# The second score product of the 64-feature heads on all 128 rows of the systolic array

## The chip, the cores and the metric

The kernel runs on one core of a Trainium2 chip. The metric is the device time of one execution in microseconds. The kernel before took 1842.69 us, the median of three runs (1839.75 to 1848.87).

## The reference

Two transformer blocks on 512 tokens of 1024 features, in 32-bit floating point. The first has four attention layers, the second a layer of four mixers, a gated feed-forward part and a last gated projection. What matters here are the scores of heads with 64 features: the sliding-window layer (16 heads), the forgetting layer (16 heads), the two attention mixers of the second block (4 heads each), and the index of the sparse attention (8 heads of 64 features that share one key).

```python
def _swa_branch(x, w_in, sinks, w_out):                    # SWA_HEAD_DIM = 64
    ...
    s = jnp.einsum('bqnkgd,bnskd->bnkgqs', q, kb, preferred_element_type=jnp.float32) * scale
    ...
def _dense_causal(q, k, v, scale, cum=None):               # forgetting layer: FOX_HEAD_DIM = 64
    ...
        s = jnp.einsum('bqhd,bkhd->bhqk', q_blk, k, preferred_element_type=jnp.float32) * scale
    ...
def dsa_mixer(q, k, v, iq, ik, iw, bias_tab):              # index: IDX_HEADS = 8, IDX_DIM = 64
    ...
        sc = jax.nn.relu(jnp.einsum("bqhd,bsd->bqhs", iqc, ik32))
        score = jnp.einsum("bqh,bqhs->bqs", iwc, sc) * idx_scale
    ...
        _, sel = lax.top_k(score, topk)                    # 128 keys of each query
```

## The kernel before, in words

Every number is split into a high part in the rounded 32-bit format that TensorE takes, and a low part, the remainder. A product of two split operands is three matmuls: high by high, high by low, low by high (`mm3`, lines 156 to 158). Activations stand feature by row: 128 features on the 128 rows, 512 tokens as columns.

A head of 64 features fills half the rows, so two of the three products share one matmul. `split_q` stacks the query of a head as high part and low part, on 64 rows each. `split_k` stacks the high part of the key twice. The first matmul of `qk_mm` (line 231) works on all 128 rows and gives high by high plus low by high. The second (line 232) gives high query by low key, and reads only the 64 rows of the high query (`r`) and of the low key. The index does the same by itself in lines 885 and 886. One score tile has 128 queries and 128 to 512 keys, so each tile takes two matmuls, and both load the same query columns as stationary operand.

The low keys lie in different places: in the sliding-window layer twice in a tile of the ring `qk` (`both=True`); in the forgetting layer once, two heads stacked, in one half of the tile `kl2` of the tag `kr`, the halves taking turns by pair of heads; in the mixers in a ring `kl` of two tiles; for the index in two tiles of `ik`. The ring `qk` has 7 tiles in the first block and also holds query and key tiles, biases (`b`) and the second half of the output weights at a layer's end.

`attend` runs one head: the score tiles go to PSUM (ring `s`, two banks), VectorE adds the bias and takes the row maxima (L396), ScalarE takes the exponential (L412), VectorE normalises (L420), TensorE transposes (L436), the result is split (L183, L184) and multiplied by the values (L445). `pairs` issues the projections of the next pair of heads ahead of the two heads at hand, so TensorE has projections (L156 to L158 into `ps_acc`) to put between the steps of the heads. In the mixers, `tick` puts 48 steps of the top-128 selection (L911, L912) into VectorE's program.

Each engine executes its list in order. The lists are written by a scheduler at build time that replays its own estimate of times, so a change of a size or of a buffer moves rows of all lists. GpSimd (POOL) takes the low parts of the weights (L138) and small steps of the norms (L318).

Of the kernel before, what the change touches and what calls it, by code (L numbers as in the profile page):

```python
# [9 lines left out]
F32 = mybir.dt.float32  # L10
R = mybir.dt.float32r
# [47 lines left out]
# output projections of the four layers and of the mixers (and of the end): PSUM banks by halves of the columns and  # L59
# token tiles, and the order of the blocks, 4 * half + tile  # L60
# [15 lines left out]
class Act:  # L76
    """Feature-major activation split exactly in two float32r parts, units of 4 blocks of 128 features."""
# [11 lines left out]
class Kern:  # L89
# [27 lines left out]
    def phase(s, ctx, tags):  # L117
        """a pool that lives as long as ctx, with its tags."""
        s.phase_pool = ctx.enter_context(s.tc.tile_pool(name="ph", bufs=1, reuse_waits="tile"))
        s.phase_tags = tags  # L120
# [9 lines left out]
    def w(s, W, k0, kn, c0, cn, th="wh", tl="wl", dve=False):  # L130
        """weights split in two parts."""
# [9 lines left out]
    def w_heads(s, W, k, c0, a, b):  # L141
        """weights of 4 heads with a + b columns each, one k tile: columns ordered [4 x a | 4 x b]."""
# [17 lines left out]
    def proj(s, W, c0, m, a, tag="acc"):  # L160
        """out^T block: (W[:, c0:c0+m])^T a."""
        out = s.p(tag)
        for u in range(0, a.n, 4):
            kn = min(4, a.n - u)
            h, l = s.w(W, u, kn, c0, m)
            for k in range(kn):
                s.mm3(out[:m], h[:, k], l[:, k], a.h(u + k), a.l(u + k), u + k == 0, u + k == a.n - 1)
        return out

    def proj_multi(s, blocks, a):  # L170
        """as proj for several (W, c0, m, tag), by halves of the tokens, so that the first halves can start before the
        second half of a is there."""
# [13 lines left out]
    def split_heads(s, ps, extra):  # L186
        """two heads of 64 rows each: a tile [high and low part] per head with the head in rows 0..63; extra(e) -> rows
        that follow, of both parts or of the high one."""
# [8 lines left out]
    def split_q(s, ps):  # L197
        """two heads of 64 rows each, stacked: [high of 0; low of 0] and [low of 1; high of 1]."""
# [10 lines left out]
    def split_k(s, ps, both=False, kl=None):  # L209
        """two heads of 64 rows each: the high part of each twice, [0; 0] and [1; 1], and the low parts [0; 1], or  # L210
        twice each like the high parts."""
        nc = s.nc
        k = s.t("qk", [P, 2, S], R)
        if both:
            kl = s.t("qk", [P, 2, S], R)
        elif kl is None:
            kl = s.t("kl", [P, S], R)
        for e, (h, l) in enumerate(HALF):
            nc.scalar.copy(k[h, e], ps[h])
            nc.scalar.copy(k[l, e], ps[h])  # L220
            low = kl[h, e] if both else kl[h]
            nc.vector.tensor_sub(low, ps[h], k[h, e].bitcast(F32))  # L222
# [4 lines left out]
    def qk_mm(s, out, i, k0, q, e, kd, kl):  # L227
        """scores of 64-row heads: (high + low of q) . high of k, and high of q . low of k."""
        mm = s.nc.tensor.matmul
        c, kk, r = slice(i * P, (i + 1) * P), slice(k0 * P, (i + 1) * P), HALF[e][0]  # L230
        mm(out, q[:, e, c], kd[:, kk], start=True, stop=False)  # L231
        return mm(out, q[r, e, c], kl[r, kk], start=False, stop=True)  # L232

# [1 line left out]
    def to_T(s, x, t, a, grp=(0, 1)):  # L235
        """token tile t of x (token-major) into a (feature-major, split)."""
# [8 lines left out]
    def bcast_row(s, row, tag):  # L245
        """a row of DRAM on every partition."""
# [5 lines left out]
    def out_units(s, W, n, half):  # L252
        """split weights of half the columns, one k tile each, in whatever is free at the end of a layer."""
# [5 lines left out]
    def pair_units(s, W, n, c0, cn, dve=False):  # L259
        """split weights of cn columns, one k tile each, both parts in a tile of the attention."""  # L260
# [15 lines left out]
    def out_proj(s, W, o, evac, banks=None, oi=5, split_last=False):  # L276
        """token-major o @ W by halves of the columns; evac(t, half, psum)."""
# [61 lines left out]
    def rms_T(s, x, t, g, a):  # L339
        """rmsnorm(x) * g of token tile t into a."""  # L340
# [9 lines left out]
    def stage_end(s, W, o, g_post, g_next, out_proj=None):  # L350
        """x += rmsnorm(o @ W) * g_post; returns rmsnorm(x) * g_next."""
# [31 lines left out]
    def attend(s, s_mm, k0s, bias, scale, v, sink=None, shift=None):  # L383
        """s_mm(out, i, k0): scores of query tile i against keys from tile k0; v(j) -> stationary [P, 128] of key
        tile j; returns the PSUM tile with the two halves of the output."""
# [65 lines left out]
    def join(s, og, e, o):  # L451
        """two halves of a head's output summed into rows 64e.. of og."""
# [97 lines left out]
    def latent(s, W, c0, n, m, g_row, xT, tag, rest=None):  # L550
        """rmsnorm of m columns of x @ W from c0 (feature-major, split); the columns up to n, transposed, into rest."""
# [27 lines left out]
    def pairs(s, order, prep, head, Wg, g0, xT, oT):  # L579
        """the pairs of heads in turn; the projections of the next pair come ahead of the two heads of one."""  # L580
# [26 lines left out]
    def v_split(s, ps, vts, f=0.5):  # L607
        """f times the token-major values of pairs of heads into [hi lo] per head; vts: [P, 2, 2, 64] per pair."""
# [10 lines left out]
    def v_proj(s, W, c0, n, a, evac, more="p", first=False):  # L619
        """token-major a @ W[:, c0:c0+n]; evac(t, psum); more: where weights wider than 256 columns go too."""  # L620
# [18 lines left out]
    def swa(s, j, li, xT, g_next):  # L639
# [8 lines left out]
        def prep(p):  # L648
# [6 lines left out]
            if pr == 0:  # L655
                K[kp] = s.split_k(kps, True)
# [16 lines left out]
    def fox(s, j, li, xT, g_next):  # L673
# [4 lines left out]
        kl2 = s.t("kr", [P, 2, S], R, name="kl2")  # L678
# [12 lines left out]
        # log sigmoid(z) = min(z, 0) - ln(1 + exp(-|z|))  # L691
# [22 lines left out]
        def prep(p):  # L714
# [17 lines left out]
            kt = s.split_k(kps or s.proj(Win, 1024 + p * P, P, xT), kl=kl2[:, p % 2])  # L732
            return qt, kt, V[g][pr], bs

        def head(d, p, e):
            q, (k, kl), v, bs = d
            return s.attend(lambda out, i, k0: s.qk_mm(out, i, k0, q, e, k[:, e], kl), [0] * T,
# [26 lines left out]
    def spill_x(s):  # L764
        """x to DRAM, for the layers whose attention needs its place."""
# [7 lines left out]
    def rel_rows(s):  # L773
        """per head 128 times the row w[511 - d] = 8 bias(d), -1e30 for the distances d < 0, in DRAM."""
# [13 lines left out]
    def rel_bias(s, h):  # L788
        """bias of head h (times 8) with the causal mask: [P, 512], key tiles i-3..i of query tile i; a row further
        down starts one element earlier."""  # L790
# [23 lines left out]
    def pool(s, W, hT, mix, b, before=None):  # L814
        """windows of one half of the channels; returns what completes it, to be called later."""
# [16 lines left out]
        # the first group of channels takes its window one doubling before the second  # L832
# [22 lines left out]
    def index_keys(s, W, hT):  # L855
        """keys and weights of the index of the sparse attention."""
        nc = s.nc
        ps, *s.iq = s.proj_multi([(W, 2304, 72, "acc"), (W, 1792, P, "acc"), (W, 1920, P, "acc")], hT)
        kh, kl = s.t("ik", [P, S], R), s.t("ik", [P, S], R)
# [13 lines left out]
    def index(s, W, hT, b):  # L873
        """what heads 2b and 2b + 1 of the index add to the scores."""
# [5 lines left out]
        for e in range(2):  # L880
            h = 2 * b + e
            for i in (1, 2, 3):
                ps = s.p("stsot"[(3 * h + i) % 5])
                c, r = slice(i * P, (i + 1) * P), HALF[e][0]
                nc.tensor.matmul(ps[:, :w[i]], q[:, e, c], kh[:, :w[i]], start=True, stop=False)
                nc.tensor.matmul(ps[:, :w[i]], q[r, e, c], kl[r, :w[i]], start=False, stop=True)
# [12 lines left out]
    def tick(s, n=1):  # L899
        """n more steps of the selection, each behind what the engine has been given so far: for one tile of queries  # L900
        the 8 best keys of those left are taken, 16 times."""
# [15 lines left out]
    def rel_prep(s, W, cq, ck, hT):  # L917
        q = s.split_q(s.proj(W, cq, P, hT))
        s.tick(4)
        k = s.split_k(s.proj(W, ck, P, hT))  # L920
# [8 lines left out]
    def rel_head(s, qk, v, h, e, og, sel=None):  # L929
# [12 lines left out]
        s.join(og, e, s.attend(lambda out, i, k0: s.qk_mm(out, i, k0, q, e, k[:, e], kl), [0] * T, bias, 0.125, s.vsel(v, e)))  # L942
# [179 lines left out]
```

## Time and profile before

| | |
|---|---|
| three runs | 1839.75, 1842.69, 1848.87 us |
| profiled execution, first to last instruction (its span) | 1840.2 us |
| time around the span in that execution | not shown by the profile; the median of the runs is 2.5 us above the span |
| TensorE busy | 1749.8 us, 95% |
| VectorE, ScalarE, GpSimd busy | 52%, 48%, 46% |
| mean granted TensorE clock | 0.976 |

The profile is that of one execution. A matmul's record starts when it, or the weight load that it must wait for, starts; its end is modelled, and records of matmuls that follow each other overlap. So a busy TensorE is not one at its peak, and the price of a matmul is read from the distance between the starts of neighbours. A weight load is a record of its own (PEld).

### The profile page before, as it was taken

Reading aid. Unit: us, or ns where it says so; the run is one execution under the profiler, and the core shown is the slowest. Engines: PE = TensorE matmul, PEld = TensorE weight load, DVE = VectorE, ACT = ScalarE, POOL = GpSimd, SP = SyncE. Lnnn points to the kernel's source line nnn. Section 1 sums busy time; section 2 is a strip of 40 time slices with the busy share of each in tenths; the row PEclk is TensorE's granted clock in tenths of the full one; section 3 lists DMA queues with packets and bytes.
Section 4 is the critical chain, followed back from the end, with each engine's and each line's share of the span. In section 5 each row is a group of like instructions: output and inputs, shape, how many; then the busy total and the mean of one; then the engine's idle time right before and its main releaser. Section 6 shows DMA issues by size and latency. Waiting matters only on the chain.

```text
span 1840.2 us, 25667 instructions
## 1 busy us (share of the span) xinstructions
PE 1749.8 (95%) x8818; PEld 1437.6 (78%) x8818; DVE 951.6 (52%) x2223; ACT 876.6 (48%) x2054; POOL 849.4 (46%) x767
## 2 busy tenths in 40 slices
PE   8999997699999999999999998998999999999999
PEld 7888776477788887777888777777778888888877
DVE  4587651367763565575477667389555222220054
ACT  4576532456635565562466653555554333332352
POOL 2645441333436554544655424545555444444571
PEclk9999999789999999999999998999999999999999
DMA  5534525422114222323354522331332333322222
GB/s 162 135 94 123 170 66 68 121 57 70 62 50 121 76 76 79 109 84 93 97 143 104 155 87 59 80 82 52 100 108 67 94 97 92 95 94 92 98 92 75
DMA packets 190203, 173.89 MB, mean 94 GB/s; under 512 B 14152, under 2 KB 154824, under 8 KB 190072
## 3 DMA queue, kind: packets, MB, share of 16 engines
q1 hardware_dynamic: 190072, 172.25, 33.4%
q8 instruction: 70, 1.15, 0.3%
q14 instruction: 61, 0.50, 0.1%
HBM read 148.31 MB, written 6.85 MB: 84 GB/s over the span
## 4 chain that ended last, share of the span: by engine, by line
PE 68%; DVE 7%; DMA 3%; POOL 3%; issue 2%; ACT 2%; SPq 0%; POOLq 0%; ACTq 0%; DVEq 0%
PE ps_acc L156 14%; PE ps_acc L157 14%; PE ps_acc L158 14%; PE ps_s L157 4%; PE ps_s L156 4%; PE ps_s L158 4%; PE ps_o L445 3%; PE ps_s L232 2%; PE ps_t L436 2%; DMA wr<-in_swa_w_in_dram 2%; PE ps_s L231 1%; DVE p L420 1%; POOL wl L138 1%; ACT p L412 1%; PE ps_t L241 1%
## 5 line engine op out<-in xcount | busy, mean ns | idle before, releaser
L138 POOL TENSOR_TENSOR wl<-wr,wh 128x512 fp32r<-128x512 f32 (+2 forms) x362 | 471.2, 1311 | 502.4 <-ACT wh L137 473.9
L137 ACT CAST wh<-wr 128x512 fp32r<-128x512 f32 (+2 forms) x368 | 223.8, 612 | 432.0 <-PE ps_acc L157 160.8
L156 PE MATMUL ps_acc<-act,wh 128*128 128x512 f32 (+1 forms) x880 | 339.1, 385 | 28.5 <-DVE qk L222 26.9
L157 PE MATMUL ps_acc<-act,wh 128*128 128x512 f32 (+1 forms) x880 | 336.5, 382 | 0.3 <-DVE act L184 0.2
L158 PE MATMUL ps_acc<-act,wl 128*128 128x512 f32 (+1 forms) x880 | 336.7, 383 | 0.0
L156 PEld LDWEIGHTS ps_acc<-act,wh 128*128 128x128 f32 x880 | 166.3, 189 | 64.1 <-issue 32.3
L158 PEld LDWEIGHTS ps_acc<-act,wl 128*128 128x128 f32 x880 | 166.0, 189 | 33.7 <-issue 1.2
L157 PEld LDWEIGHTS ps_acc<-act,wh 128*128 128x128 f32 x880 | 166.4, 189 | 31.9 <-issue 0.9
L412 ACT ACTIVATE p<-p,st 128x256 f32<-128x256 f32 (+3 forms) x288 | 153.5, 537 | 32.0 <-DVE st L403 17.6
L156 PE MATMUL ps_acc<-wh,act 128*128 128x256 f32 (+3 forms) x384 | 132.2, 344 | 6.1 <-ACT act L462 3.1
L184 DVE TENSOR_TENSOR ptl<-ps_t,pth 128x512 fp32r<-128x512 f32 (+1 forms) x200 | 117.1, 596 | 36.1 <-ACT pth L183 35.5
L183 ACT CAST pth<-ps_t 128x512 fp32r<-128x512 f32 (+1 forms) x200 | 99.8, 516 | 74.8 <-PE ps_t L436 64.5
L420 DVE TENSOR_SCALAR p<-p,st 128x256 f32<-128x256 f32 (+3 forms) x264 | 129.1, 546 | 1.8
L158 PE MATMUL ps_acc<-wh,act 128*128 128x256 f32 (+3 forms) x384 | 129.8, 338 | 0.0
L157 PE MATMUL ps_acc<-wl,act 128*128 128x256 f32 (+3 forms) x384 | 128.5, 335 | 0.0
L436 PE MATMUL ps_t<-c_ident,p 128*128 128x128 f32 x672 | 112.3, 277 | 7.8 <-DVE p L420 6.0
L436 PEld LDWEIGHTS ps_t<-c_ident,p 128*128 128x128 f32 x672 | 79.8, 140 | 22.6 <-DVE p L420 8.6
L445 PE MATMUL ps_o<-pth,v 128*128 128x256 f32 (+3 forms) x288 | 90.2, 319 | 4.0 <-DVE og L456 2.7
L445 PE MATMUL ps_o<-ptl,v 128*128 128x256 f32 (+3 forms) x288 | 87.5, 333 | 3.4 <-DVE ptl L184 3.4
L156 PEld LDWEIGHTS ps_acc<-wh,act 128*128 128x128 f32 x384 | 76.5, 199 | 14.6 <-ACT act L462 3.3
L157 PEld LDWEIGHTS ps_acc<-wl,act 128*128 128x128 f32 x384 | 76.2, 198 | 5.3 <-issue 0.5
L158 PEld LDWEIGHTS ps_acc<-wh,act 128*128 128x128 f32 x384 | 76.0, 198 | 5.2 <-DVE act L184 0.2
(370 smaller groups left out, 3807.0 us busy)
## 6 DMA issues: line engine op xcount, KB each, us to landing
wr<-in_w_gate_up_dram SPq DMA_DIRECT2D x88, 256.0 KB, 2.9
wr<-in_fox_w_in_dram SPq DMA_DIRECT2D x60, 256.0 KB, 3.0
wr<-in_w_in_dram SPq DMA_DIRECT2D x48, 256.0 KB, 2.8
wr<-in_w_down_dram SPq DMA_DIRECT2D x44, 256.0 KB, 2.6
wr<-in_swa_w_in_dram SPq DMA_DIRECT2D x40, 256.0 KB, 3.1
wr<-in_mla_w_in_dram SPq DMA_DIRECT2D x32, 256.0 KB, 3.2
qk<-qk SPq DMA_DIRECT2D x32, 256.0 KB, 3.2
wr<-in_mla_w_out_dram SPq DMA_DIRECT2D x32, 256.0 KB, 3.5
```

The costliest lines, as they stand in the source:

```text
L137: nc.scalar.copy(h, raw)
L138: (nc.vector if dve else nc.gpsimd).tensor_sub(l, raw, h.bitcast(F32))
L156: mm(out, lh, rh, start=first, stop=False)
L157: mm(out, lh, rl, start=False, stop=False)
L158: return mm(out, ll, rh, start=False, stop=last)
L183: s.nc.scalar.copy(hi, src)
L184: s.nc.vector.tensor_sub(lo, src, hi.bitcast(F32))
L232: return mm(out, q[r, e, c], kl[r, kk], start=False, stop=True)
L412: nc.scalar.activation(a, a, AF.Exp, bias=st[:, 1, i:i + 1], scale=scale, accum_out=st[:, 2, i:i + 1])
L420: nc.vector.tensor_scalar_mul(a, a, st[:, 3, i:i + 1])
L436: nc.tensor.transpose(ps[:, n:n + P], sc[:, c:c + P], s.ident)
L445: nc.tensor.matmul(o[:, j * P:j * P + m], vj, pp[:, c:c + m], start=first, stop=k == 1 and grp[-1] == max(2, grp[-1]) and j == grp[-1], sk ...
```

## The change

The second matmul now reads all 128 rows of the query tile, and of a low-key tile of full height. In the sliding-window layer and for the index the low keys stand twice already, so the product of the low parts comes in as well. In the forgetting layer and the mixers the other 64 rows are zeros, written once per tile by a new function, `low_tile`. For these tiles the forgetting layer takes the tag `kr` and one more tile of the ring `qk`, for its whole length. In the mixers the ring `kl` has two tiles of twice the width; the index's keys take the first, and the second low-key tile can be had when the index is done. Comments and docstrings go too, which shifts line numbers.

```diff
@@ split_k, qk_mm @@
+    def low_tile(s, tag):
+        t = s.t(tag, [P, 2, S], R, name="kl2")
+        for e, (h, l) in enumerate(HALF):
+            s.nc.gpsimd.memset(t[l, e].bitcast(F32), 0.0)
+        return t
-    def split_k(s, ps, both=False, kl=None):
+    def split_k(s, ps, kl=None):
...
+        both = kl is None
         if both:
             kl = s.t("qk", [P, 2, S], R)
-        elif kl is None:
-            kl = s.t("kl", [P, S], R)
...
-            low = kl[h, e] if both else kl[h]
-            nc.vector.tensor_sub(low, ps[h], k[h, e].bitcast(F32))
+            nc.vector.tensor_sub(kl[h, e], ps[h], k[h, e].bitcast(F32))
...
         mm(out, q[:, e, c], kd[:, kk], start=True, stop=False)
-        return mm(out, q[r, e, c], kl[r, kk], start=False, stop=True)
+        return mm(out, q[:, e, c], kl[:, kk], start=False, stop=True)
@@ fox @@
-        kl2 = s.t("kr", [P, 2, S], R, name="kl2")
+        kl2 = [s.low_tile(g) for g in ("kr", "qk")]
...
-            kt = s.split_k(..., kl=kl2[:, p % 2])
+            kt = s.split_k(..., kl=kl2[p % 2])
@@ index_keys, index @@
-        kh, kl = s.t("ik", [P, S], R), s.t("ik", [P, S], R)
+        kh, kl = s.parts(s.t("kl", [P, 2, S], R, name="ik"))
...
-                nc.tensor.matmul(ps[:, :w[i]], q[r, e, c], kl[r, :w[i]], start=False, stop=True)
+                nc.tensor.matmul(ps[:, :w[i]], q[:, e, c], kl[:, :w[i]], start=False, stop=True)
@@ mixers @@
         for b in range(4):
             s.index(W, hT, b)
+        kl2 = [s.low_tile("kl") for _ in range(2)]
```

The number of matmuls, and of instructions on VectorE and ScalarE, stays; GpSimd gets eight memsets of 64 rows by 512 columns. Three places of the lists show what moves.

TensorE in the second half of the sliding-window layer, before: the two products of one score tile are L231 and L232, L445 is the output product, L436 the transposes, L156 to L158 projections.

```order
L158 MATMUL ps_acc<-act,wl 128x512
L445 MATMUL ps_o<-pth,v 128x256
L231 MATMUL ps_s<-qk 128x256
L232 MATMUL ps_s<-qk 128x256
L231 MATMUL ps_s<-qk 128x256
L445 MATMUL ps_o<-ptl,v 128x256
L445 MATMUL ps_o<-pth,v 128x256
```

The same place in the change (the two products are L237 and L238 there, the output product L451):

```order
L158 MATMUL ps_acc<-act,wl 128x512
L237 MATMUL ps_s<-qk 128x256
L451 MATMUL ps_o<-pth,v 128x256
L238 MATMUL ps_s<-qk 128x256
L237 MATMUL ps_s<-qk 128x256
L238 MATMUL ps_s<-qk 128x256
L156 MATMUL ps_acc<-act,wh 128x512
L157 MATMUL ps_acc<-act,wh 128x512
L451 MATMUL ps_o<-ptl,v 128x256
```

The second score tile is finished ahead of the rest of the output product, and a piece of a projection stands between; elsewhere in this layer rows move by a few places in the same manner.

GpSimd at the end of the sliding-window layer, in the change: L138 are low parts of the forgetting layer's first weights, L213 the memsets of its low-key tile in the ring `qk`, L324 and L336 steps of the layer norm.

```order
L138 TENSOR_TENSOR wl<-wr,wh 128x272
L138 TENSOR_TENSOR p<-wr,p 128x272
L213 MEMSET kl_5376 64x512 x2
L324 TENSOR_TENSOR mv<-mv,small 128x1
L336 TENSOR_TENSOR x<-x,ckv 128x1024
L324 TENSOR_TENSOR mv<-mv,small 128x1
```

The two memsets are new; the rows around them stand as before. They wait for the third matmul of the last block of the output projection, which frees the tile.

GpSimd in the index, in the change: L901 adds the index scores of a head to the sum from which the selection starts, L213 are the memsets of the second low-key tile of the mixers.

```order
L901 TENSOR_TENSOR sel<-f,sel 128x512
L138 TENSOR_TENSOR wl<-wr,wh 128x512
L901 TENSOR_TENSOR sel<-f,sel 128x256
L213 MEMSET kl_12162 64x512 x2
L901 TENSOR_TENSOR sel<-f,sel 128x384
L138 TENSOR_TENSOR wl<-wr,wh 128x512
L901 TENSOR_TENSOR sel<-f,sel 128x512
```

Here too only the memsets are new. They wait for the last matmul of the index, and stand ahead of two of the last three adds.

## Rows read from the trace of the kernel before

**Rows 1.** The page: busy time by engine, and the chain that ended last by engine.

```profile
PE 1749.8 (95%) x8818; PEld 1437.6 (78%) x8818; DVE 951.6 (52%) x2223; ACT 876.6 (48%) x2054; POOL 849.4 (46%) x767
...
PE 68%; DVE 7%; DMA 3%; POOL 3%; issue 2%; ACT 2%; SPq 0%; POOLq 0%; ACTq 0%; DVEq 0%
```

**Rows 2.** Second products of the attention, line 232: shape, count, duration min/median/max in ns.

```profile
L232 PE MATMUL ps_s<-kl,qk x96: 322/435/579, 585.1 to 1349.6; 64*128 64x512 f32 x24, 64*128 64x384 f32 x24, 64*128 64x256 f32 x24, 64*128 64x128 f32 x24
...
L232 PE MATMUL ps_s<-qk x64: 322/380/579, 343.1 to 496.5; 64*128 64x256 f32 x48, 64*128 64x128 f32 x16
```

**Rows 3.** Busy time by stretch of the index's second products, line 886: PE, PEld.

```profile
1164.00:1202.00 38.00, 10.47 (x24) 4.38 (x24) 1.00 0.28 70
```

**Rows 4.** TensorE in order of time, sliding-window layer: start, duration, line, shape.

```profile
348.80 0.28 PE L231 MATMUL ps_s<-qk 128*128 128x256 f32 x1
349.00 0.38 PE L232 MATMUL ps_s<-qk 64*128 64x256 f32 x1
349.31 0.50 PE L156 MATMUL ps_acc<-act,wh 128*128 128x512 f32 x1
349.65 0.40 PE L157 MATMUL ps_acc<-act,wh 128*128 128x512 f32 x1
```

**Rows 5.** Matmuls and weight loads in order of time, index.

```profile
1167.23 0.19 PEld L885 LDWEIGHTS ps_t<-ik,qk 128*128 128x128 f32 x1
1167.46 0.28 PE L885 MATMUL ps_t<-ik,qk 128*128 128x256 f32 x1
...
1167.67 0.18 PEld L886 LDWEIGHTS ps_t<-ik,qk 64*128 64x128 f32 x1 [0.25 <-issue]
...
1169.56 0.19 PEld L156 LDWEIGHTS ps_acc<-act,wh 128*128 128x128 f32 x1 [0.24 <-issue]
...
1169.90 0.39 PE L157 MATMUL ps_acc<-act,wh 128*128 128x512 f32 x1
```

**Rows 6.** TensorE in order of time, fourth layer: scores of 96-row heads.

```profile
925.81 0.40 PE L158 MATMUL ps_s<-qk 96*128 96x512 f32 x1
926.05 0.33 PE L156 MATMUL ps_s<-qk 96*128 96x384 f32 x1
926.22 0.34 PE L157 MATMUL ps_s<-qk 96*128 96x384 f32 x1
...
927.28 0.28 PE L156 MATMUL ps_s<-qk 96*128 96x256 f32 x1
927.40 0.28 PE L157 MATMUL ps_s<-qk 96*128 96x256 f32 x1
```

**Rows 7.** Busy time by stretch: PE, PEld, DVE, ACT, POOL, TensorE clock, DMA.

```profile
342.00:498.00 156.00, 153.13 (x699) 117.09 (x698) 102.87 (x314) 91.06 (x242) 55.73 (x44) 0.95 0.23 68
584.00:810.00 226.00, 223.62 (x1138) 177.98 (x1137) 132.87 (x338) 127.66 (x303) 122.77 (x124) 0.98 0.32 91
880.00:1060.00 180.00, 175.30 (x974) 151.14 (x973) 119.00 (x328) 109.03 (x308) 91.22 (x95) 1.00 0.45 120
1164.00:1202.00 38.00, 38.00 (x143) 24.55 (x142) 16.71 (x26) 25.88 (x51) 20.48 (x19) 1.00 0.28 70
1202.00:1300.00 98.00, 91.26 (x439) 71.96 (x439) 90.11 (x241) 46.69 (x109) 45.46 (x41) 0.97 0.27 72
1300.00:1352.00 52.00, 49.25 (x215) 36.50 (x214) 30.50 (x67) 30.90 (x73) 33.74 (x29) 1.00 0.32 102
```

**Rows 8.** Groups of instructions on GpSimd by line: a memset, an add on 64 rows.

```profile
L820 POOL MEMSET bd<- 128x128 f32 x2 | 0.4, 204 | 0.0
...
L839 POOL TENSOR_TENSOR pad<-pad 64x512 f32<-64x512 f32 x2 | 2.3, 1158 | 0.2
```

**Rows 9.** Busy time by stretch, columns as in Rows 7, sliding-window layer.

```profile
390.00:394.00 4.00, 4.00 (x10) 3.09 (x10) 2.52 (x10) 2.69 (x10) 0.00 (x0) 0.50 0.00 0
```

**Rows 10.** TensorE in order of time in that stretch.

```profile
390.64 0.63 PE L156 MATMUL ps_acc<-act,wh 128*128 128x512 f32 x1
391.07 0.63 PE L157 MATMUL ps_acc<-act,wh 128*128 128x512 f32 x1
```

More of the change, by code (lines that the diff above doesn't have):

```diff
@@ L229, in qk_mm @@
         mm = s.nc.tensor.matmul
-        c, kk, r = slice(i * P, (i + 1) * P), slice(k0 * P, (i + 1) * P), HALF[e][0]
+        c, kk = slice(i * P, (i + 1) * P), slice(k0 * P, (i + 1) * P)
         mm(out, q[:, e, c], kd[:, kk], start=True, stop=False)
-        return mm(out, q[r, e, c], kl[r, kk], start=False, stop=True)
+        return mm(out, q[:, e, c], kl[:, kk], start=False, stop=True)
     def to_T(s, x, t, a, grp=(0, 1)):
@@ L655, in prep @@
             if pr == 0:
-                K[kp] = s.split_k(kps, True)
+                K[kp] = s.split_k(kps)
             win = s.t("rope", [P, 2, 256], name="win")
@@ L731, in prep @@
             qt = s.split_q(qps or s.proj(Win, p * P, P, xT))
-            kt = s.split_k(kps or s.proj(Win, 1024 + p * P, P, xT), kl=kl2[:, p % 2])
+            kt = s.split_k(kps or s.proj(Win, 1024 + p * P, P, xT), kl=kl2[p % 2])
             return qt, kt, V[g][pr], bs
@@ L736, in head @@
             q, (k, kl), v, bs = d
-            return s.attend(lambda out, i, k0: s.qk_mm(out, i, k0, q, e, k[:, e], kl), [0] * T,
+            return s.attend(lambda out, i, k0: s.qk_mm(out, i, k0, q, e, k[:, e], kl[:, e]), [0] * T,
                             lambda i: bs[e][i], 0.125, s.vsel(v, e), shift=cq[:, :, 2 * p + e])
@@ L883, in index @@
                 ps = s.p("stsot"[(3 * h + i) % 5])
-                c, r = slice(i * P, (i + 1) * P), HALF[e][0]
+                c = slice(i * P, (i + 1) * P)
                 nc.tensor.matmul(ps[:, :w[i]], q[:, e, c], kh[:, :w[i]], start=True, stop=False)
-                nc.tensor.matmul(ps[:, :w[i]], q[r, e, c], kl[r, :w[i]], start=False, stop=True)
+                nc.tensor.matmul(ps[:, :w[i]], q[:, e, c], kl[:, :w[i]], start=False, stop=True)
                 rl = s.t("f", [P, S])
@@ L915, in tick, with rel_prep @@
                 nc.vector.tensor_scalar(sc, sc, -2e38, NEG, op0=ALU.is_gt, op1=ALU.mult)
-    def rel_prep(s, W, cq, ck, hT):
+    def rel_prep(s, W, cq, ck, hT, kl):
         q = s.split_q(s.proj(W, cq, P, hT))
         s.tick(4)
-        k = s.split_k(s.proj(W, ck, P, hT))
+        k = s.split_k(s.proj(W, ck, P, hT), kl)
         s.tick(4)
@@ L940, in rel_head @@
             bias = lambda i: bb[:, off[i]:off[i] + (i + 1) * P] if i else b[:, 384:]
-        s.join(og, e, s.attend(lambda out, i, k0: s.qk_mm(out, i, k0, q, e, k[:, e], kl), [0] * T, bias, 0.125, s.vsel(v, e)))
+        s.join(og, e, s.attend(lambda out, i, k0: s.qk_mm(out, i, k0, q, e, k[:, e], kl[:, e]), [0] * T, bias, 0.125, s.vsel(v, e)))
     def mixers(s, hT):
@@ L955, in prep @@
         def prep(c0, pr):
-            return s.rel_prep(W, c0 + pr * P, c0 + 256 + pr * P, hT)
+            return s.rel_prep(W, c0 + pr * P, c0 + 256 + pr * P, hT, kl2[pr])
         s.index_keys(W, hT)
@@ L1090 @@
 PH1 = dict(cqt=1, f=4, p=2, pth=2, ptl=2, qk=7, qr=1, cq=2, ckv=2, rope=2, kr=1, gq=1)
-PH2 = dict(kl=2, f=6, p=2, pth=2, ptl=2, v=3, qk=4, rb=2, cw=6, pad=3, bd=2, ik=2, iw=1, sel=1, sb=1, m8=3)
+PH2 = dict(kl=2, f=6, p=2, pth=2, ptl=2, v=3, qk=4, rb=2, cw=6, pad=3, bd=2, iw=1, sel=1, sb=1, m8=3)
 PH3 = dict(f=6, p=2, hid=6, hid2=2, sel=1, sb=1)
```

## Prediction

> **What bounds the kernel now.** I read the page first: TensorE is busy 95% of the span, and 68% of the chain that ended last is TensorE's [rows 1]. So the matmuls that the change touches stand on the engine that sets the end. How many there are comes from the instructions of line 232: 160 are recorded, 96 with a low key of its own tile and 64 with one in `qk` [rows 2]. The loops give 64 in the sliding-window layer, 64 in the forgetting layer and 32 in the mixers; the 24 of the index stand in a stretch of their own [rows 3]. That makes 184.
>
> Next I read TensorE in order of time around a single score tile in a stream of projections [rows 4]. Its first product starts at 348.80, the second at 349.00, the projection behind it at 349.31, the next at 349.65: 0.85 us for two matmuls of 256 columns and one of 512. The reader is to compare this with full streams. In the fourth layer, whose scores have 96 rows, a matmul of 512 columns is followed after 0.24 us (925.81 to 926.05), one of 384 after 0.17 (926.05 to 926.22), one of 256 after 0.12 (927.28 to 927.40) [rows 6]. By these the three matmuls take 0.12 + 0.12 + 0.24 = 0.48 us. The single tile pays 0.37 us that no other score pays.
>
> Where this goes is seen with the weight loads beside the matmuls, in the index [rows 5]. The load for L885 (128 rows) starts at 1167.23 and the matmul at 1167.46: loaded while the matmul ahead was at work. The load for L886 (64 rows) starts at 1167.67, 0.25 us after the load engine went idle, which ended "issue": no semaphore held it. The load of 128 rows behind the last of them (1169.56) again stood idle for 0.24 us. [...] The stretch from 1167.46 to 1169.90 holds three pairs (256, 384 and 512 columns) and a projection: 2.44 us, against 2 x (0.12 + 0.17 + 0.24) + 0.24 = 1.30 in a full stream. That is 1.14 for three, 0.38 each, as much as the single tile paid. The scores with 96 rows stand between matmuls of 128 without any of this, so it is the half height, not the score, that costs.
>
> Last I read the busy time of the engines by stretch [rows 7], to see where a faster TensorE would wait for another.
>
> **The change part by part.** The change makes the second product full in height; its columns, and so its own time, stay. What goes is 0.38 us for each of 184: 184 x 0.38 = 70 us, of which 64 x 0.38 = 24.3 in the sliding-window layer, as much in the forgetting layer, 24 x 0.38 = 9.1 in the index, and 16 x 0.38 = 6.1 in each half of the mixers (before and behind 1300).
>
> How much of it reaches the end, by stretch [rows 7]:
>
> Sliding window (342 to 498): TensorE is busy 153.1 of 156 us, VectorE 102.9. Without 24.3 us VectorE would be busy 102.9 / 132 = 78%. The nearest row for a stretch without half-height matmuls is that of the fourth layer (880 to 1060): there VectorE is busy 66%, and TensorE stands still 4.7 of 180 us, 2.6%. With 78% I take 7% of 132 = 9.2 us, 6.3 more than the 2.9 now. Gain 24.3 - 6.3 = 18. Ends: nothing lost (24), or VectorE and its chains set the pace and 10 remain.
>
> Forgetting layer (584 to 810): VectorE would be busy 132.9 / 202 = 66%, just as in the fourth layer. 2.6% of 202 = 5.3 us, 2.9 more than the 2.4 now. Gain 21, ends 16 and 24.
>
> Index (1164 to 1202): TensorE has no gap. ScalarE, which takes every score out of PSUM, would be busy 25.9 / 29 = 89%, so I let it take back a third: gain 6, ends 3 and 9.
>
> Mixers up to 1300: VectorE is busy 90.1 of 98 us with the selection, TensorE has 6.7 us of gaps. What the 16 matmuls there give becomes more gaps. Gain 0.5, ends 0 and 3. Mixers from 1300: VectorE and ScalarE are at 59%; I take 4.5 of 6.1, ends 2 and 6.
>
> Sum: 18 + 21 + 6 + 0.5 + 4.5 = 50 us. Ends: 10 + 16 + 3 + 0 + 2 = 31 and 24 + 24 + 9 + 3 + 6 = 66.
>
> What it adds: eight memsets of 64 x 512 on GpSimd. No row shows that shape. A memset of 128 x 128 takes 0.2 us, an add on 64 x 512 takes 1.16 [rows 8]; the new ones write four times the columns of the one and read nothing, unlike the other, so I take 0.6 each, 5 us in all, with 2 and 9 as ends. Two stand among weights in the sliding-window layer, where GpSimd is busy 56 of 156 us: hidden. Two wait at the end of that layer for the third matmul of the last output block; behind them stands the norm's step for the third token tile, which needs the block before and some VectorE steps, and TensorE has the first two tiles' projections to do meanwhile: hidden, or some 2 us if these run out. Two stand among the weights ahead of the index: hidden. Two stand ahead of the last adds of the index, from which the selection starts, and VectorE is the bound behind it: here 1.2 us count. I take 2.5 us of loss for all eight, ends 0 and 6.
>
> The tile that the forgetting layer takes from the ring `qk` leaves six for the biases, queries and keys of two pairs, three each. In the list every split of a new query or key still waits for nothing but its own projection; I cost it at nothing, and at 5 us if a split comes late once per two pairs (four times a projection's piece of five matmuls, 5 x 0.24 us). Below nothing it can't go, since no wait disappears. The rows that move in TensorE's list move by a few places in either direction: nothing, plus or minus 4 us, which is a stall of the size seen in the sliding-window layer now (2.9 us), with a margin.
>
> So 50 - 2.5 = 47.5 us less, 1840.2 - 47.5 = 1792.7 for the span. The median of the runs stands 2.5 us above the span, and I add these: 1795 us. The likeliest case's own range: 62 less (1780) to 31 less (1812).
>
> **The rivals.** *The other engines eat it.* TensorE gets to its matmuls sooner but the row maxima, exponentials and transposes of one head follow each other, and the lists put only so many projections between. Then only the forgetting layer gains (18), the sliding-window layer 6, the index and the rest 2: 26 less, 1817 us. For it: in 342 to 498 four fifths of the time would be VectorE's. Against: now TensorE waits there 2.9 us in all, and 180 us of the fourth layer lose only 4.7.
>
> *Rows don't matter: no gain.* If the 0.38 us came from two products with the same stationary operand, or from the wait for the second operand, it would stay: 1842.7 us plus up to 6 for the memsets, 1845. Against it stand the 96-row scores: L156 and L157 there share a stationary operand too, and follow after 0.17 us [rows 6]. [...]
>
> [...]
>
> **How the numbers follow.** The forecast 0.77, the other engines 0.14, no gain 0.05, slower by the clock 0.04. The low end is 1778, two below the likeliest case's, for a higher clock in the sliding-window layer (now 0.95 [rows 7]). The high end is 1818, which takes in the second case's middle. A measurement of this kernel can tell about 0.5%, 9 us, from no change. Faster than 1833.5: the first two cases, 0.91. Within: 0.05. Slower than 1852: 0.04.
>
> **What would show it right or wrong.** In the profile after: the second products with 128 rows; a single tile of 256 columns in a stream of projections 0.24 us long (from its first product to the projection behind), and no load that begins idle by "issue" behind a score; TensorE's busy time lower by some 60 us; gaps of TensorE in 342 to 498 grown to about 9 us and in the mixers before 1300 by about 6. Wrong: loads that still start idle behind a second product, or a sliding-window stretch that keeps more than 147 us.

## The result, and the profile after

The changed kernel takes 1801.0 us (1800.6 to 1803.1, four runs) against 1843.5 us for the kernel before on the same chip (1839.8 to 1848.9, four runs): a ratio of 0.977, interval 0.975 to 0.979. The forecast was 1795 us. The profiled execution spans 1799.1 us, 41.1 less than before.

The page's busy line and its chain by engine, for [rows 1]:

```profile
PE 1695.6 (94%) x8818; PEld 1429.8 (79%) x8818; DVE 959.6 (53%) x2223; ACT 873.9 (49%) x2054; POOL 853.9 (47%) x775
...
PE 51%; DVE 9%; ACT 3%; POOL 2%; issue 2%; DMA 1%; SPq 0%; ACTq 0%; POOLq 0%; DVEq 0%
```

TensorE gave up 54 us of busy time, the span only 41. The shares of the chain can't be set against each other: before, the profile follows it back to 277 us, after, only to 583 us, so that the sliding-window layer is missing from it (the shares add up to 85% of the span before and to 68% after).

The second products by instruction, for [rows 2]: the first is the forgetting layer, the second the sliding-window layer, each with min/median/max in ns, first and last start; then one of three groups of the index:

```profile
L238 PE MATMUL ps_s<-kl,qk x64: 218/335/628, 578.3 to 790.2; 128*128 128x512 f32 x16, 128*128 128x384 f32 x16, 128*128 128x256 f32 x16, 128*128 128x128 f32 x16
...
L238 PE MATMUL ps_s<-qk x64: 273/281/415, 345.6 to 488.7; 128*128 128x256 f32 x48, 128*128 128x128 f32 x16
...
L892 PE MATMUL ps_t<-ik,qk x10: 276/340/404, 1140.7 to 1165.3; 128*128 128x256 f32 x4, 128*128 128x512 f32 x4, 128*128 128x384 f32 x2
```

All have 128 rows. The first and last starts give the lengths that are compared below. A single tile in a stream of projections, as in [rows 4] (start, duration, line, shape):

```profile
350.96 0.28 PE L237 MATMUL ps_s<-qk 128*128 128x256 f32 x1
351.08 0.28 PE L238 MATMUL ps_s<-qk 128*128 128x256 f32 x1
351.20 0.40 PE L156 MATMUL ps_acc<-act,wh 128*128 128x512 f32 x1
351.43 0.39 PE L157 MATMUL ps_acc<-act,wh 128*128 128x512 f32 x1
```

The three matmuls take 0.47 us where [rows 4] had 0.85. The weight loads of the index, for [rows 5]:

```profile
1140.33 0.19 PEld L891 LDWEIGHTS ps_t<-ik,qk 128*128 128x128 f32 x1
1140.57 0.19 PEld L892 LDWEIGHTS ps_t<-ik,qk 128*128 128x128 f32 x1
...
1141.16 0.19 PEld L892 LDWEIGHTS ps_o<-ik,qk 128*128 128x128 f32 x1
1141.40 0.19 PEld L156 LDWEIGHTS ps_acc<-act,wh 128*128 128x128 f32 x1
```

No load of the index stands idle by "issue" any more, into the second product or out of it; before, 22 of the 24 loads of L886 had stood idle by it, 5.6 us in all. Busy time by stretch, for [rows 7] (PE, PEld, DVE, ACT, POOL, TensorE clock, DMA): sliding window, forgetting layer, index, mixers in two parts:

```profile
345.00:489.00 144.00, 134.33 (x690) 110.99 (x690) 107.89 (x310) 89.40 (x240) 54.90 (x43) 0.95 0.25 74
578.00:790.00 212.00, 206.72 (x1142) 177.45 (x1141) 132.75 (x343) 128.38 (x308) 120.03 (x122) 0.98 0.35 96
1137.00:1161.00 24.00, 24.00 (x122) 20.30 (x121) 13.62 (x19) 19.81 (x42) 17.63 (x16) 1.00 0.38 99
1161.00:1257.00 96.00, 90.09 (x447) 74.50 (x446) 91.24 (x246) 49.99 (x115) 47.32 (x44) 0.95 0.29 75
1257.00:1311.00 54.00, 49.77 (x223) 39.62 (x222) 31.48 (x68) 30.98 (x70) 35.48 (x31) 0.94 0.31 98
```

TensorE is idle for 9.7 of 144 us in the sliding-window layer, where [rows 7] had 2.9 of 156. Where the 41 us came from, by first and last start of the second products:

| stretch | before | after | difference | forecast |
|---|---|---|---|---|
| sliding window, first to last | 343.1 to 496.5 | 345.6 to 488.7 | -10.3 | -18 |
| forgetting, first to last | 585.1 to 812.2 | 578.3 to 790.2 | -15.2 | -21 |
| index, first to last | 1167.7 to 1201.1 | 1140.7 to 1165.3 | -8.8 | -6 |
| last of the index to last of the mixers | 1201.1 to 1349.6 | 1165.3 to 1310.1 | -3.7 | -5 |
| all the rest | | | -3.1 | +2.5 |

### The profile page after: what moved, and what is told of

The parts are those of the page before. It is cut to its first block, busy times and chain, and to the rows that moved or that the text cites. A ratio compares the mean times of both kernels' runs of the same rounds, so it can differ in the third digit from the quotient of the medians.

```text
span 1799.1 us, 25682 instructions
## 1 busy us (share of the span) xinstructions
PE 1695.6 (94%) x8818; PEld 1429.8 (79%) x8818; DVE 959.6 (53%) x2223; ACT 873.9 (49%) x2054; POOL 853.9 (47%) x775
## 4 chain that ended last, share of the span: by engine, by line
PE 51%; DVE 9%; ACT 3%; POOL 2%; issue 2%; DMA 1%; SPq 0%; ACTq 0%; POOLq 0%; DVEq 0%
PE ps_acc L156 11%; PE ps_acc L157 10%; PE ps_acc L158 10%; PE ps_s L156 4%; PE ps_s L157 4%; PE ps_s L158 4%; PE ps_o L451 2%; PE ps_t L442 2%; DVE p L426 1%; ACT p L418 1%; DVE sel L918 1%; DVE m L917 1%; DVE p L402 1%; DVE ptl L184 1%; PE ps_s L237 1%
## 5 line engine op out<-in xcount | busy, mean ns | idle before, releaser
L138 POOL TENSOR_TENSOR wl<-wr,wh 128x512 fp32r<-128x512 f32 (+2 forms) x362 | 471.1, 1312 | 460.0 <-ACT wh L137 444.9
L156 PE MATMUL ps_acc<-act,wh 128*128 128x512 f32 (+1 forms) x880 | 335.8, 382 | 27.8 <-DVE qk L227 26.9
L158 PE MATMUL ps_acc<-act,wl 128*128 128x512 f32 (+1 forms) x880 | 334.1, 380 | 0.0
L156 PEld LDWEIGHTS ps_acc<-act,wh 128*128 128x128 f32 x880 | 165.8, 188 | 58.6 <-issue 27.3
L158 PEld LDWEIGHTS ps_acc<-act,wl 128*128 128x128 f32 x880 | 165.5, 188 | 31.1
L156 PE MATMUL ps_acc<-wh,act 128*128 128x256 f32 (+3 forms) x384 | 131.8, 343 | 7.3 <-ACT act L468 3.1
L426 DVE TENSOR_SCALAR p<-p,st 128x256 f32<-128x256 f32 (+3 forms) x264 | 132.7, 561 | 1.8
L442 PE MATMUL ps_t<-c_ident,p 128*128 128x128 f32 x672 | 117.5, 283 | 16.7 <-DVE p L426 12.5
L158 PE MATMUL ps_acc<-wh,act 128*128 128x256 f32 (+3 forms) x384 | 128.8, 336 | 0.1
L442 PEld LDWEIGHTS ps_t<-c_ident,p 128*128 128x128 f32 x672 | 82.3, 143 | 33.8 <-DVE p L426 14.0
L451 PE MATMUL ps_o<-pth,v 128*128 128x256 f32 (+3 forms) x288 | 90.0, 318 | 6.2 <-DVE og L462 4.2
L451 PE MATMUL ps_o<-ptl,v 128*128 128x256 f32 (+3 forms) x288 | 88.3, 335 | 4.8 <-DVE ptl L184 4.5
L156 PEld LDWEIGHTS ps_acc<-wh,act 128*128 128x128 f32 x384 | 75.9, 198 | 15.7 <-ACT act L468 3.3
L158 PEld LDWEIGHTS ps_acc<-wh,act 128*128 128x128 f32 x384 | 75.3, 196 | 5.2 <-DVE act L184 0.3
```

Of the source, the lines that this page charges most:

```text
L138: (nc.vector if dve else nc.gpsimd).tensor_sub(l, raw, h.bitcast(F32))
L156: mm(out, lh, rh, start=first, stop=False)
L158: return mm(out, ll, rh, start=False, stop=last)
L426: nc.vector.tensor_scalar_mul(a, a, st[:, 3, i:i + 1])
L442: nc.tensor.transpose(ps[:, n:n + P], sc[:, c:c + P], s.ident)
L451: nc.tensor.matmul(o[:, j * P:j * P + m], vj, pp[:, c:c + m], start=first, stop=k == 1 and grp[-1] == max(2, grp[-1]) and j == grp[-1], sk ...
```

## The experiments

**Each part alone.** Four kernels are the one before with one part of the change. In the index this is the edit of one line, in the sliding-window layer of three (a flag that is handed to `qk_mm`); the other two bring the tiles of full height with them.

```
sliding window:  q[r, e, c], kl[r, kk]     ->  q[:, e, c], kl[:, kk]      (this layer's scores only)
forgetting:      kl2 of the tag kr         ->  two tiles by low_tile, all rows in this layer's scores
index:           q[r, e, c], kl[r, :w[i]]  ->  q[:, e, c], kl[:, :w[i]]
mixers:          kl of half height         ->  two tiles by low_tile, all rows in the mixers' scores
```

> Of the change only the sliding-window layer: its 64 second products read 128 rows. Theory (each step to 64 rows and back costs 0.38 us, 24 us for 64; the profile of the full change has this layer 10.5 us shorter): about 10 us less than before, ratio 0.994, and no other stretch shorter. Rival (the layer's 10.5 us came from elsewhere, as a moved row or a spread between executions): ratio within 0.002 of 1. The prediction's own term was 18 us, ratio 0.990.

> Of the change only the forgetting layer, with its two zeroed tiles, one of them from the ring qk. Theory: 64 steps, 24 us of TensorE time, of which the full change showed 15 to 17 at the end: ratio 0.991. Rival (the tile taken from the ring, and the memsets, cost several us that the other layers' gain hides): ratio 0.995 or more.

> Of the change only the index: 24 second products on 128 rows, no memset. Theory: 9 us of TensorE time; the full change showed 8.7 of them in the stretch of the index, and the selection behind it starts earlier by as much: 9 us less, ratio 0.995. Rival (ScalarE, which takes the scores out of PSUM, takes back a third, as the prediction had it): 6 us less, ratio 0.997.

> Of the change only the two attention mixers, with the zeroed tiles (and the index's keys in the first of them). Theory: 12 us of TensorE time, but the 16 products ahead of the end of the selection stand where VectorE is busy nine tenths of the time: 4 to 5 us less, ratio 0.9975. Rival (TensorE sets the pace there after all): 10 to 12 us less, ratio 0.994. Other rival (memsets and moved rows eat it): ratio 1.

| part alone | median us | ratio | interval |
|---|---|---|---|
| sliding window | 1829.2 | 0.9920 | 0.9888 to 0.9953 |
| forgetting | 1828.4 | 0.9911 | 0.9880 to 0.9942 |
| index | 1831.0 | 0.9929 | 0.9899 to 0.9959 |
| mixers | 1837.1 | 0.9972 | 0.9950 to 0.9994 |

The kernel before took 1843.9 us beside them (17 runs). The four differences are 14.8, 15.5, 12.9 and 6.8 us, 50 in all against 42.5 for the whole; each is uncertain by 4 to 6 us, so whether the parts get in each other's way can't be said. Each interval holds the ratio of its theory (0.994, 0.991, 0.995, 0.9975) and none of a rival's; in the sliding-window layer it holds the prediction's own 0.990 too. The traces are sharper than the medians. The second products of the sliding-window layer alone, of the forgetting layer alone, and of the index alone:

```profile
L232 PE MATMUL ps_s<-qk x64: 273/281/415, 343.3 to 485.7; 128*128 128x256 f32 x48, 128*128 128x128 f32 x16
```

```profile
L238 PE MATMUL ps_s<-kl,qk x64: 218/335/527, 591.0 to 800.9; 128*128 128x512 f32 x16, 128*128 128x384 f32 x16, 128*128 128x256 f32 x16, 128*128 128x128 f32 x16
```

```profile
L886 PE MATMUL ps_t<-ik,qk x10: 276/340/404, 1165.8 to 1190.4; 128*128 128x256 f32 x4, 128*128 128x512 f32 x4, 128*128 128x384 f32 x2
```

These are 142.4, 209.9 and 24.6 us, within 2 us of what the whole change has there. So in these three each gain arises in the stretch whose rows were changed. The edits of the sliding-window layer and of the index change nothing but the number of rows: they add no tile and no memset. The mixers are not as clear. Alone they take 143.8 us from the last product of the index to their own last one, against 148.5 before; but the next kernel, whose mixers keep the half height, has 144.0 us there.

**Half-height products in groups.** If a step between heights is what costs, three half-height products in a row should pay for it once. The kernel is the one before, with the index's products in another order:

```
for i in (1, 2, 3): matmul(three[i], q[:, e, c], kh, start=True, stop=False)
for i in (1, 2, 3): matmul(three[i], q[r, e, c], kl[r], start=False, stop=True)
```

> The kernel before, but in the index the 128-row products of three score tiles are written first and then their three 64-row products. In TensorE's list the 24 products of 64 rows then stand in 16 groups of one, two or three. Theory (the cost is the step between heights): a 64-row product behind a 64-row product follows after its plain distance, 0.12, 0.17 or 0.24 us by its columns, plus at most a weight load, and the index as a whole loses about 16 x 0.38 = 6.1 us instead of 9.1. Rival (every 64-row matmul costs 0.38 us by itself): inside a group the distances are as long as before, 0.31 to 0.42 us, and the loss stays 9.1 us.

One execution gave 1841.4 us, which alone tells no difference. The scheduler put the 24 products into 16 groups. TensorE in order of time around a group of three (L886 on 128 rows, L889 on 64):

```profile
1172.07 0.28 PE L886 MATMUL ps_t<-ik,qk 128*128 128x256 f32 x1
1172.19 0.34 PE L886 MATMUL ps_s<-ik,qk 128*128 128x384 f32 x1
1172.37 0.40 PE L886 MATMUL ps_o<-ik,qk 128*128 128x512 f32 x1
1172.70 0.38 PE L889 MATMUL ps_t<-ik,qk 64*128 64x256 f32 x1
1172.92 0.33 PE L889 MATMUL ps_s<-ik,qk 64*128 64x384 f32 x1
1173.10 0.39 PE L889 MATMUL ps_o<-ik,qk 64*128 64x512 f32 x1
1173.42 0.50 PE L156 MATMUL ps_acc<-act,wh 128*128 128x512 f32 x1
1173.75 0.40 PE L157 MATMUL ps_acc<-act,wh 128*128 128x512 f32 x1
```

From 1172.07 to 1173.75 there are 1.68 us; at full-stream distances, 2 x (0.12 + 0.18 + 0.24) + 0.24, it would be 1.32. The three pay 0.36 together, not each. The second half-height product follows the first after 0.22, the third the second after 0.18: as fast as 384 columns on 128 rows (1172.19 to 1172.37). The half height in itself is as fast; the change from one height to the other cost 0.09 on the way in, 0.08 on the way out, and 0.1 more for the matmul behind each. Over the whole index the distances beside a half-height product hold 4.9 us beyond full-stream ones here, against 7.7 in the kernel before: 0.31 and 0.32 a visit. The index got only 1.1 us shorter (32.3 us instead of 33.4), since the new order has 125 matmuls in it where 117 were.

The loads show the same two places. The load engine stood idle by "issue" for 0.31 us ahead of the first half-height load of the group (1172.70), and for 0.31 ahead of the load of 128 rows behind it (1173.41); the second and the third half-height load follow the one ahead after 0.11 us, without that idle time. What TensorE does meanwhile no row shows; the visit of this group to the other height cost 0.36 us.

**VectorE in the sliding-window layer.** Two kernels change who normalises the probabilities there. The first leaves it out, so that the layer's result is not normalised; the second gives two of four query tiles to GpSimd, as the mixers do with one:

```
-            how = ("vvvv" if "cq" in s.phase_tags else "aavp")[i]
+  first:    how = (...)[i] if sink is None else ""          # and  elif how:  for the last case
+  second:   how = (...)[i] if sink is None else "vvpp"[i]
```

> The changed kernel without the normalisation of the probabilities in the sliding-window layer (64 VectorE multiplications of about 0.55 us, 35 us in all, left out; the layer's output is then not normalised). Theory (in that layer VectorE's part of each head is what TensorE now waits for): the layer, 143 us long in the changed kernel, loses 10 to 15 us: ratio to before 0.969 to 0.972, against 0.977 for the change. Rival (the order of TensorE's list, or ScalarE's exponentials, set the pace): under 4 us, ratio 0.975 or more.

> The changed kernel, with two of the four normalisations per head of the sliding-window layer on GpSimd (32 x 0.75 to 0.86 us, GpSimd is busy 58 of 146 us there) instead of VectorE. Theory (VectorE's load sets the pace): 3 to 8 us less than the changed kernel, ratio to before 0.973 to 0.9755. Rival (the length of the chain within a head sets the pace, and GpSimd, slower and in order behind weights, makes it longer): no gain or slower than the changed kernel, ratio 0.977 to 0.981.

The first took 1784.2 us, a ratio of 0.9682 (0.9660 to 0.9704), the second 1789.1 us, 0.9696 (0.9663 to 0.9729). What TensorE waited for from 340 to 500 us: in all, times, longest. The kernel before, then the change:

```profile
PE ps_s L231 <- DVE st L396: 1.4, 2, 1.2
PE ps_o L445 <- DVE og L456: 0.5, 1, 0.5
...
PE ps_t L436 <- DVE p L420: 0.2, 1, 0.2
```

```profile
PE ps_s L237 <- DVE st L402: 4.0, 3, 1.6
PE ps_t L442 <- DVE p L426: 4.0, 8, 0.9
PE ps_o L451 <- DVE og L462: 0.9, 1, 0.9
```

The transposes (L442) wait for the normalisation (L426), and the next scores (L237) for VectorE to read the last ones out of PSUM (L402). The busy time of the layer without normalisation, and with half of it on GpSimd:

```profile
348.00:474.00 126.00, 123.82 (x683) 103.56 (x681) 76.56 (x245) 88.41 (x238) 53.85 (x42) 1.00 0.27 83
```

```profile
344.00:482.00 138.00, 130.85 (x683) 109.46 (x682) 93.35 (x278) 89.15 (x239) 72.31 (x72) 0.95 0.25 76
```

Without it the layer's second products run from 347.7 to 474.6, 126.9 us instead of 143.1, TensorE is idle for 2.2 us, and the granted clock is 1.00. Part of the 16.2 us is the clock's. In the trace of the change the granted clock is 1.00 or 0.50: from 467 to 471 us it is 0.50, and projections follow after 0.43 us (469.07 to 469.50), where at 1.00 they follow after 0.24 (472.48 to 472.72). By this, at a mean of 0.95, some 14 of 143 us ran at 0.50, which costs at most 7 us, an estimate (half of it). At least 9 us are left to the steps of VectorE that each head waits for, so these held the layer up, and not the matmuls alone. Shared, it is 138.6 us (343.9 to 482.5) at the same clock of 0.95, and all that the layer computes is kept: faster than the change. Of the 12 us between the medians the profiled execution shows 4.5 in this layer.

**The stall ahead of the sliding-window layer.** In both kernels TensorE stands still for 26.9 us, until 338 us before and 341 after (there: [26.86 <-DVE qk L227]). SP's queue has there one write of the relative biases (L792: 8 rows of 640 to 1024 places in DRAM), then the gains and the first weights. The DMAs of the changed kernel from 270 to 345 us: in 40 slices the busy tenths of 16 engines and GB/s, and issues with count, KB each, and median time to landing:

```profile
DMA  0000244754444444466574444474445458797544
GB/s 0 0 0 0 33 48 51 151 87 51 48 51 48 52 46 52 48 125 122 62 119 50 51 48 51 48 122 46 52 46 53 46 122 319 215 271 209 167 128 140
...
rel<-p SPq DMA_DIRECT2D x1, 2560.0 KB
cq<-in_ln_g_dram SPq DMA_DIRECT2D x1, 512.0 KB, 50.0
ckv<-in_ln_b_dram SPq DMA_DIRECT2D x1, 512.0 KB, 49.0
```

For 53 us the engines move some 50 GB/s for most of the time, and the gains land after 50 us. One kernel puts the write on ScalarE's queue (`nc.scalar.dma_start(s.rel, ...)`):

> The changed kernel, with the write of the relative-position rows to memory (1024 pieces of 2560 bytes, at the end of the first layer) issued by ScalarE instead of SyncE. In both profiles TensorE stands still for 26.9 us at the start of the sliding-window layer; the weights it waits for stand in one queue behind that write. Theory (the queue is what blocks): weights in another queue share the engines with it, and 15 to 25 us go: ratio to before 0.963 to 0.969. Rival (the write holds the DMA engines or the memory itself): the stall stays, ratio 0.977.

It took 1795.9 us, 0.9746 (0.9721 to 0.9770), less of a gain than the theory had. The wait in its trace, and its issues in the same stretch:

```profile
PE ps_acc L156 <- DVE qk L227: 23.7, 1, 23.7
```

```profile
rel<-p ACTq DMA_DIRECT2D x1, 2560.0 KB
cq<-in_ln_g_dram SPq DMA_DIRECT2D x1, 512.0 KB, 20.5
ckv<-in_ln_b_dram SPq DMA_DIRECT2D x1, 512.0 KB, 21.6
```

The gains land sooner, but the stall is still 23.7 us. So the place in SP's queue was at most a small part of the cause. The next kernels keep SP's queue, write the eight rows to DRAM once, and from there the 128 places of each head, one head behind each pair's mask in the program; the second also has the shared normalisation:

```
-        nc.sync.dma_start(s.rel, r.rearrange(...).to_broadcast([8, P, 640]))
+        nc.sync.dma_start(s.rel_src, r)                       # 8 x 640 in DRAM
+    def rel_piece(s, h):                                      # called in the layer's prep(p)
+        s.nc.sync.dma_start(s.rel[h:h + 1], s.rel_src[h:h + 1].rearrange(...).to_broadcast([1, P, 640]))
```

> The changed kernel, but the 1024-piece write of the relative biases is no longer one transfer ahead of the sliding-window layer's weights: the 8 x 640 table goes to DRAM once, and from there the eight heads' rows are written one head at a time (128 pieces each), one behind the mask of each pair of heads in that layer. In the changed kernel TensorE stands still for 26.9 us until 341.1, because the first weights come through behind and between the pieces of that write; with the write on ScalarE's queue the stall was still 23.7 us, and the weights landed at the same slow pace until the write was over. Theory: it is the write's traffic, not its place in a queue, that holds the weights back. Then the stall falls to under 5 us and the time to 1776-1782 (0.963 to 0.967 of the kernel before). Rival 1: the pieces now hold back the loads inside the sliding-window layer, eight times a few us, and the layer from first to last score grows from 143 us by as much as the stall shrinks: 1795 to 1802. Rival 2: the first weights are late for another reason: the stall stays above 20 us, and the time at about 1800.

> The write in eight pieces as in the run before, together with the normalisation of two of the four query tiles of each sliding-window head on GpSimd instead of VectorE. The second alone gave 1789.1 against 1801.0 for the changed kernel, 12 us. If both terms add, 12 us below the run before: 1764 to 1770 (0.957 to 0.960 of the kernel before). If the sliding-window layer is held by its loads once the write is in pieces, the two do not add and it ends within 5 us of the run before.

They took 1771.3 us, 0.9618 (0.9578 to 0.9659), and 1761.3 us, 0.9551 (0.9504 to 0.9599), both some us below the times expected: the two gains add, 30 and 10 us. The second is the fastest kernel here, 4.5% below the one before. The DMAs' busy tenths (of 16 engines) and rates in the first from 270 to 305 us, and its issues:

```profile
DMA  0000001006898999999999508572846755000000
GB/s 0 0 0 0 0 0 23 0 26 217 199 348 234 269 301 255 342 363 398 380 362 337 178 8 219 145 218 48 250 145 201 232 156 171 9 0 0 19 0 0
...
rel<-rel_src SPq DMA_DIRECT2D x8, 320.0 KB, 6.1
wr<-in_swa_w_in_dram SPq DMA_DIRECT2D x7, 256.0 KB, 2.9
cq<-in_ln_g_dram SPq DMA_DIRECT2D x1, 512.0 KB, 7.8
```

TensorE has no wait for L227 in this trace at all, and the layer stays at 143.0 us (314.4 to 457.4). But the reason is not the one expected. The scheduler issued all eight pieces at once, from 276.4 us on, so nothing was spread; from DRAM the write was over in about 10 us, while the engines moved 200 to 400 GB/s, the gains among it, where from eight partitions of SBUF it took 53. Both writes are 1024 pieces of 2560 bytes. From SBUF each packet took 392 ns, which over 53 us is 7.6 of them under way at a time; from DRAM it was at most some 160 ns, an estimate: the busy tenths from 278 to 290 us add up to 164 us of the engines' time, the gains among it. There 8 or 9 tenths of the 16 engines were busy for most of the write. So the packets from SBUF themselves were slow, and only about half of the 16 engines had one at a time. The new write differs in its source and also in its shape, eight transfers of one head; which of the two brought the other engines in was not tried apart. What held the weights back was thus the slow write: beside it the gains took 50 us to land, on a queue apart from it 20.5, and 7.8 where it was fast.

## Why the prediction was right, and where it was off

*The mechanism: right.* The step between heights goes (0.47 us for the single tile, forecast 0.48), loads run ahead again, and both the edits that change rows alone and the grouped index show that it is the step and not the second product that costs. The rival by which rows don't matter falls. In the load itself the rows hardly show (0.18 us for 64, 0.19 for 128 [rows 5]); in the distances between starts they do (0.85 us [rows 4] against 0.47 for the three matmuls). The prices hold: 8.8 us over the 24 products of the index are 0.37 each, forecast 0.38.

*The sliding-window layer: mis-sized.* The step that failed is "With 78% I take 7% of 132 = 9.2 us, 6.3 more than the 2.9 now. Gain 24.3 - 6.3 = 18". The idle time came out as forecast, 9.7 us, but the gain is 10.3, at the very end of the bounds of 10 to 24. At 0.37 a tile 23.5 us went, so 13 came back, twice the 6.3. The view of busy time shows half of it (idle 2.9 to 9.7). The rest is an estimate from the starts of the layer's matmuls: the distances beyond those of a full stream, without the ones beside a half-height product or at a clock of 0.50, grew from 10.7 to 19.1 us; of the 10.7 some 4 still belong to the step (64 x 0.06, the part of 0.37 that falls on the matmul behind). So waits went from 6.7 to 19.1, and what the clock of 0.50 costs from 5.2 to 5.8: 13.0 together. With slightly other distances for a full stream each figure moves by some 2 us. A wait can lie inside a record, which starts with the load that the matmul must wait for (in the index before, load and matmul of a second product both at 1167.67), and the idle time misses it. What I should have taken as the limit is VectorE's chain within each head, as the kernel without normalisation shows, and not its busy share. The stretch of 143 us is still below the 147 that would have meant wrong.

*The forgetting layer: somewhat less,* 15.2 instead of 21, just below the bounds of 16 to 24. By the same estimate, waits went from 5.0 to 11.9 us and the clock of 0.50 from 2.6 to 3.9, 8.2 of the 23.5. VectorE's share was about as forecast (132.75 of 212, 63% for 66%); the fourth layer was probably too kind a model, since its waits, too, were read as idle time.

*The index: more,* 8.8 instead of 6. I let ScalarE take back a third; it was busy 19.8 of 24 us and took nothing back.

*The mixers: right in sum by luck,* 3.7 of 5, but the wrong way round. The last step of the selection divides them (before, then the change), and a wait of TensorE that of the two only the kernel before has:

```profile
L912 DVE MATCH_REPLACE8 sel<-m,sel x48: 397/541/686, 1201.9 to 1296.7; 128x256 f32<-128x256 f32 x16, 128x384 f32<-128x384 f32 x16, 128x512 f32<-128x512 f32 x16
...
L918 DVE MATCH_REPLACE8 sel<-m,sel x48: 399/540/686, 1166.7 to 1254.8; 128x256 f32<-128x256 f32 x16, 128x384 f32<-128x384 f32 x16, 128x512 f32<-128x512 f32 x16
...
PE ps_acc L849 <- POOL pad L835: 4.3, 1, 4.3
```

From the last product of the index to the last step of the selection it was 95.6 us and is 89.5, 6.1 less where 0.5 was forecast; TensorE's gaps there did not grow by 6 us (6.7 of 98 before, 5.9 of 96 after). About 4 us of this may be the wait for GpSimd's `pad`, which is gone: it is gone in the kernel with the grouped index too, whose mixers keep the half height, and there this part takes 91.5 us. Why it went stays open. From the end of the selection to the last product it was 52.9 us and is 55.3, 2.4 more where 4.5 less were forecast. The granted clock fell there from 1.00 [rows 7] to 0.94, so that some 6.5 of 54 us ran at 0.50; by an estimate half of that, about 3 us, is lost by it. The rest stays open.

*The memsets: cheaper.* They take 0.52 us each (forecast 0.6), and TensorE waits for none; the 2.5 us of loss did not show. That, 3 us between the stretches, which single executions don't tell from spread, and the index offset 8.4 us of the 13.5 by which the two layers fell short. That the sum came so close, 41.1 of 47.5 us in the span, is in this part luck. The range of the likeliest case, 62 to 31 less, is not worked out in the prediction: its ends add up to 31 and 66 before the memsets and the moved rows. The 41 lies inside either.

*The other rivals.* That the other engines eat the gain is partly so: it holds for more than half of the gain in the sliding-window layer, for a third in the forgetting layer and not for the index. A kernel slower by the clock, to which the prediction gives 0.04, did not come: the clock's mean over the execution was 0.976 and is 0.975, and in the sliding-window layer it is 0.95 in both; but in the mixers it fell (0.97 to 0.95 and 1.00 to 0.94), at a price of a few us by the estimate above.

## What to carry to other kernels

Look at the distances between starts, not at the duration of the matmuls: a short matmul on 64 rows in a full stream of 128-row ones cost more by its two steps (0.37 us) than by its columns (0.12 to 0.24). Zeros in the empty half took that back (0.47 us for the three matmuls of a single tile instead of 0.85), and grouping by height a part of it (4.9 us beyond full-stream distances in the index instead of 7.7). Before counting such a gain in full, ask which chain of the other engines runs beside it: where VectorE had three quarters of the stretch (107.9 of 144 us), more than half of the gain came back, by the estimate nearly all of it as waits, many of them inside records that count as busy (idle time grew by 6.8 us, the waits by 12.4). And read the longest single wait first: one slow transfer cost as much as two thirds of the whole change gave.

## What the runs showed of the hardware that was not expected

- In the streams read here a visit of TensorE to 64 rows among matmuls of 128 cost 0.36 to 0.38 us, whether one matmul was made there (0.37 [rows 4], 0.38 [rows 5]) or three (0.36), and 0.32 on the mean of the index; 96 rows among 128 cost nothing that shows (in the kernel before, matmuls of 256, 384 and 512 columns are followed after 0.12, 0.18 and 0.23 us, the medians, where the rows change from 128 to 96 or back, and after 0.12, 0.17 and 0.23 us where they stay at 128).
- A write from eight partitions of SBUF took 53 us for its 2.62 MB, 49 GB/s; while the same bytes came from DRAM, the engines moved 200 to 400 GB/s, the gains among it; both writes were on SP's queue. A packet of 2560 bytes took 392 ns in the one and, by the estimate above, at most some 160 ns in the other. What set the rate of the first, no run here tried.
- Beside the slow write, loads on another queue were slow too (20.5 us to landing on a queue that had no part in the write, 7.8 once it was fast).
- In the sliding-window layer the granted clock rose from 0.95 to 1.00 when VectorE's normalisation was left out. With it shared it was 0.95 in one kernel and 0.99 in the other, the one with the write in pieces, whose layer took 134.0 us instead of 138.6; what it was that lifted it was not tried apart.
